# One buffer moved into the weight ring, and a fallback branch that loads its weights in small pieces

## The chip, the core and the metric

The kernel runs on one core of a Trainium2 chip. The metric is the time of one execution on the device in microseconds (us); the kernel before takes 759.27 us, the median of 3 runs (758.9 to 759.5).

## What is computed

A trunk of two layers works on one sequence of 256 tokens with 1024 features, all in float32. Each layer is a token mixer followed by a mixture of experts (MoE), both behind an RMS norm and a modulation by a conditioning vector. Layer 0 mixes with chunked gated linear attention, layer 1 with a gated recurrent block. A router picks two of 16 experts for each token:

```python
for i in range(DEPTH):                       # 2 layers
    sh1, sc1, g1, sh2, sc2, g2 = jnp.split(cond @ ada_w[i] + ada_b[i], 6, axis=-1)
    h = modulate(rmsnorm(x, norm_mix_g[i]), sh1, sc1)
    x = x + g1[:, None] * mixer_i(h)         # gla_mixer or lru_mixer
    h = modulate(rmsnorm(x, norm_ffn_g[i]), sh2, sc2)
    x = x + g2[:, None] * grouped_moe(h, router_w, router_bias, ...)
return rmsnorm(x, final_norm_g)

# grouped_moe, after the choice of two experts per token:
for e in range(N_EXPERTS):                   # 16
    he = jax.nn.silu(t @ w_gate[e]) * (t @ w_up[e])
    out = out + combine[:, e:e + 1] * (he @ w_down[e])
```

Every weight is used once, so some 285 MB have to come from HBM.

## The kernel before

**The ring.** Weights come in pieces of 1 MB (128 partitions x 2048 floats). SP (SyncE) issues them one after the other, in the order in which they are used, into a pool `ring` of `SLOTS = 17` buffers (slots). `Stream` hands them out: `ahead(n)` emits the transfers up to piece n, `get` first calls `ahead(at + look)` and then returns the next piece. A piece's transfer can be issued when a slot is free, that is when the last reader of an earlier piece is done. Some activations live in slots too (`big(...)`: `v`, `S`, `sg`, `oT`, `xp`, `xc`, `xg` and so on), so `look` leaves room for them: 13 in the mixers, 15 in the MoE. The framework that the kernel is written in chooses the slot of each tile, orders each engine's instructions and writes all semaphores.

**`h` and `hT`.** `new_h` makes the normed activations `h` (tokens in partitions) and their transpose `hT` (8 KB in each partition, exactly a slot's size), each in a buffer of its own in the pool `wk`. `hT` is read by the projections of the mixer, and in `out_route` it holds the transposed x from which `logits` computes the router (L830); behind the last `logits` only the overflow branch reads it.

**One layer.** The mixer runs, then `out_route`: output projection, norm, router, and `route_order`, which ranks the experts by their token counts. The ranking (`r_ordi`, L951) is read into registers of SP; before that only the weights of two experts with fixed places (unit `u0`, 12 pieces) can be transferred. `moe` then works through seven units: six with two experts and 12 pieces each, and the last one with four experts and 24 pieces. A unit does `up_proj` (gate and up, L1030), `down_proj` (L1041; in the last unit `down_part`, L1052) and `scatter` (L1060, L1061).

**The overflow branch.** Each expert has a fixed number of places for tokens. If some expert got more tokens than places, `overflow` repairs the sum. It is called once in each layer, in the sixth unit (`u == len(UNITS) - 2`). SP reads the flag behind the last transfer emitted by then (`issue_after(mark["load"])`), and every engine compares and branches (L1067). In the body a loop over 16 experts loads whole halves of the three weights into `h` (six transfers of 1 MB on SP in one pass) and computes with `hT`. On the measured inputs the flag is 0 in both layers and the body is skipped. An `If` is a barrier to the order: nothing behind it in the program goes ahead of it on the same engine.

**The completion counters.** SP's transfers use eight semaphores in turn, one for each transfer in order; a transfer's counter is full when all its data has landed. Where a branch is skipped, each engine still has to bring the counters that the body would have raised to the values that the code behind the branch expects. For a transfer counter of the body, the skipping path on SP holds one instruction: it waits until the transfers issued before on that counter have landed, and adds what the body would have added.

Of the kernel before, what the change touches and what calls it, by code (L numbers as in the profile page):

```python
# [14 lines left out]
P = 128  # L15
# [20 lines left out]
]  # L36
NS = 2
ND = NE - NS
SLOTS = 17
HALVES = [slice(0, 512), slice(512, 1024)]  # L40

TAIL = [(slice(0, 512), 0), (slice(512, 768), 0), (slice(768, 1024), 1024)]
# [33 lines left out]
def trunk(ctx, tc, I, out):  # L76
# [5 lines left out]
    wk = ctx.enter_context(tc.tile_pool(name="wk", bufs=1))  # L82
    sm = ctx.enter_context(tc.tile_pool(name="sm", bufs=2))
    pp = ctx.enter_context(tc.tile_pool(name="pp", bufs=8, space=PSUM))
    stream = Stream(ring, SLOTS - 4)

    def bank():
        return pp.tile([P, 512], F32, name="ps")

    def big(name):  # L90
        return ring.tile([P, 2048], F32, name="w")

    def mid(name):
        return wk.tile([P, 1024], F32, name="mid", tag="mid", bufs=3)
# [313 lines left out]
        return rsqrt(ss)  # L408

    def new_h():  # L410
        return wk.tile([P, NM, D], F32, name="h"), wk.tile([P, 8, S], F32, name="hT")

    def scaled(h, m, r):

# [45 lines left out]
    def out_route(l, yT, gate, gs, rest=None, last=None):  # L460

        w = [stream.get("o").rearrange("p (j n) -> p j n", j=2) for _ in range(4)]
        stream.look = SLOTS - 2
        h, hT = new_h()
        R = route_begin()

        def part(m, hf, between={}):
            sl = slice(hf * 512, (hf + 1) * 512)
            ps = bank()
            for k in range(8):  # L470
                if k in between:
                    between[k]()
                T.matmul(ps, yT[:, k, m * P:(m + 1) * P], w[k // 2][:, k % 2, sl], start=k == 0, stop=k == 7)  # L473
            tmp = s2("tmp")
            V.tensor_mul(tmp, ps, gate[:, sl])
            b = V.tensor_add(x[:, m, sl], x[:, m, sl], tmp)
            mark["x"] = b.ins

        def first():
            turn_h(x, hT, 0, halves=[1])  # L480
            stats_of[0] = stats(0)
            scaled(h, 0, stats_of[0])

        late = len(jobs) > 2
        stats_of = [None, None]
        with tc.manual_schedule(engines={T.engine}):
            part(0, 0)
            part(0, 1, {3: lambda: turn_h(x, hT, 0, halves=[0])})
            if rest:
                rest()  # L490
            router(R, gs)
            part(1, 0, {2: lambda: settle(2), 4: first, 6: lambda: router_shift(R, gs[1], 0), 7: lambda: logits(R, hT, 0)})
            router_shift(R, gs[1], 1)
            scores(R, 0, stats_of[0])
            choose(R, 0)
            fill(2)
            part(1, 1, {3: lambda: turn_h(x, hT, 1, halves=[0]), 5: lambda: logits(R, hT, 1, halves=[0]),
                        7: lambda: route_count(R, 0)})
            stream.ahead(stream.at + SLOTS - 1)
            r = stats(1)  # L500
            if late:
                accs = mid("acc")
                fill_now(accs[:, 0:512])
            else:
                settle(1)
            turn_h(x, hT, 1, halves=[1])
            xg, oh = gather_begin(R)
            gather_tile(R, h, oh, 0, 0, [0])
            logits(R, hT, 1, halves=[1])
            scores(R, 1, r)  # L510
            scaled(h, 1, r)
            gather_tile(R, h, oh, 0, 0, [1, 2, 3])
            choose(R, 1)
            gather_tile(R, h, oh, 0, 1)
            route_count(R, 1)
            if late:
                fill_now(accs[:, 512:1024])
            else:
                settle(1)
            if last:  # L520
                last()
            gather_end(l, R, h, xg, gs)
        R["xg"] = xg
        return h, hT, R
# [468 lines left out]
    def moe(l, h, hT, R, gs, g2, done=None):  # L993
# [69 lines left out]
        def overflow():  # L1063

            with tc.issue_after(mark["load"]):
                flag = nc.values_load(R["flag"][0:1, 0:1], min_val=0, max_val=1)
            with tc.If(flag > 0):  # L1067
                bent_before = mark["bent"]
                for m in range(NM):
                    turn_h(h, hT, m, gs)  # L1070
                mark["bent"] = bent_before
                co = sm.tile([P, NM, NE], F32, name="o_co", bufs=1)
                c2 = sm.tile([P, NM, NE], F32, name="o_c2", bufs=1)
                for m in range(NM):
                    V.tensor_scalar(co[:, m], R["oh"][:, m, 0], R["wv"][:, m, 0:1], None, op0=OP.mult)
                    V.scalar_tensor_tensor(c2[:, m], R["oh"][:, m, 1], R["wv"][:, m, 1:2], co[:, m],
                                           op0=OP.mult, op1=OP.add)
                V.tensor_mul(co, c2, R["ov"])
                with tc.For_i(0, NE, 1) as e:
                    def load(name, n, j, q):  # L1080
                        t = h.rearrange("p m n -> p (m n)")
                        nc.sync.dma_start(t, I[name][l][ds(e, 1), q * n:(q + 1) * n, :]
                                          .rearrange("o (p j) n -> (o p) (j n)", j=j))
                        return t.rearrange("p (j n) -> p j n", j=j)

                    cc = sm.tile([P, NM], F32, name="o_cc", bufs=1)
                    V.tensor_copy(cc[:, :, None], co[:, :, ds(e, 1)])
                    pgu = []
                    for name in ("moe_w_gate", "moe_w_up"):
                        pm = [bank() for _ in range(NM)]  # L1090
                        for q in range(2):
                            w = load(name, 512, 4, q)
                            for m in range(NM):
                                for j in range(4):
                                    k = 4 * q + j
                                    T.matmul(pm[m], hT[:, k, m * P:(m + 1) * P], w[:, j], start=k == 0, stop=k == 7)
                        pgu.append(pm)
                    aTs = []
                    am, tm = mid("o_act"), mid("o_aT")
                    for m in range(NM):  # L1100
                        act = am[:, m * DE:(m + 1) * DE]
                        A.activation(act, pgu[0][m], AF.Silu)
                        V.tensor_mul(act, act, pgu[1][m])
                        ps = bank()
                        av = act.rearrange("t (b p j) -> t b j p", b=2, j=2)
                        for k in range(4):
                            T.transpose(ps[:, k * P:(k + 1) * P], av[:, k // 2, k % 2, :], ident)
                        aT = tm[:, m * DE:(m + 1) * DE].rearrange("p (k t) -> p k t", k=4)
                        A.copy(aT, ps.rearrange("p (k t) -> p k t", k=4))
                        aTs.append(aT)  # L1110
                    py = [[bank() for _ in range(2)] for _ in range(NM)]
                    for q in range(2):
                        w = load("moe_w_down", 256, 2, q)
                        for m in range(NM):
                            for hf in range(2):
                                for j in range(2):
                                    k = 2 * q + j
                                    T.matmul(py[m][hf], aTs[m][:, k], w[:, j, hf * 512:(hf + 1) * 512],
                                             start=k == 0, stop=k == 3)
                    for m in range(NM):  # L1120
                        for hf in range(2):
                            sl = slice(hf * 512, (hf + 1) * 512)
                            tmp = am[:, hf * 512:(hf + 1) * 512]
                            V.scalar_tensor_tensor(tmp, py[m][hf], cc[:, m:m + 1], g2[:, sl], op0=OP.mult, op1=OP.mult)
                            V.tensor_add(x[:, m, sl], x[:, m, sl], tmp)

        xg = R["xg"]
        with tc.issue_after(mark["bent"]):
            route_end(R, *R["order"])
        pend = None  # L1130
        for u, unit in enumerate(UNITS):
            y = mid("y")
            t0 = (u - 1) % 2 * P if u else 0
            if u == len(UNITS) - 2:
                scatter(*pend)
                pend = None
                overflow()
            pg = up_proj(unit, xg, t0)
            if u:
                settle()  # L1140
# [49 lines left out]
    h, hT, R = out_route(0, oT, g1, gf, rest)  # L1190
    ss0 = sm.tile([P, 3, NM], F32, name="ss3", bufs=1)
    moe(0, h, hT, R, gf, g2, done=lambda q: last_squares(q, ss0))
    stream.look = SLOTS - 4
    h, hT = norm(rsqrt2(ss0), gn)
    g1 = gate_vec(1, 0)
    gf = scale_shift(1, 1)
# [52 lines left out]
```

## Time and profile of the kernel before

| | |
|---|---|
| time, median of 3 runs | 759.27 us (758.9 to 759.5) |
| time of the profiled execution | 757.96 us |
| its span, first to last instruction | 756.2 us |
| TensorE busy / VectorE busy / ScalarE busy | 93% / 45% / 17% |
| HBM read over the span | 284.54 MB, mean 379 GB/s with the rest |

The profile covers one execution. Its span is cut into 40 equal slices; for each slice a digit tells how busy an engine or the transfer engines were, and a line gives the GB/s that the transfers moved. Matmuls are pipelined, so a busy TensorE is not one at its peak. "DMA share" is the mean busy share of the 16 transfer engines; it can be a little over 1.

### The profile page before, as it was taken

Reading aid. Unit: us, or ns where it says so; the run is one execution under the profiler, and the core shown is the slowest. Engines: PE = TensorE matmul, PEld = TensorE weight load, DVE = VectorE, ACT = ScalarE, POOL = GpSimd, SP = SyncE. Lnnn points to the kernel's source line nnn. Section 1 sums busy time; section 2 is a strip of 40 time slices with the busy share of each in tenths; the row PEclk is TensorE's granted clock in tenths of the full one; section 3 lists DMA queues with packets and bytes.
Section 4 is the critical chain, followed back from the end, with each engine's and each line's share of the span. In section 5 each row is a group of like instructions: output and inputs, shape, how many; then the busy total and the mean of one; then the engine's idle time right before and its main releaser. Section 6 shows DMA issues by size and latency. Waiting matters only on the chain. (4 is left out here: it accounts for less than half of the span.)

```text
span 756.2 us, 9538 instructions
## 1 busy us (share of the span) xinstructions
PE 699.6 (93%) x3559; PEld 342.8 (45%) x3559; DVE 340.4 (45%) x780; ACT 131.4 (17%) x257; POOL 27.4 (4%) x69
## 2 busy tenths in 40 slices
PE   4899899999999999999887999998999999999874
PEld 3345745454633533533226888655433433433212
DVE  3626983897413223231023589996523143140214
ACT  5006112122200000000013166123210010010002
POOL 5000001000000000000000014000000000000000
PEclk9999999999999999999999999999999999999998
DMA  9999999779999999999999999991999999999994
GB/s 304 384 386 387 386 396 386 269 318 384 423 370 422 421 421 420 423 409 422 411 363 379 381 367 350 406 377 59 423 421 419 419 421 421 421 420 410 422 373 150
DMA packets 80445, 286.27 MB, mean 379 GB/s; under 512 B 5991, under 2 KB 16280, under 8 KB 57866
## 3 DMA queue, kind: packets, MB, share of 16 engines
q1 hardware_dynamic: 78752, 284.71, 96.0%
q10 hardware_dynamic: 1258, 0.66, 0.3%
q8 instruction: 30, 0.49, 0.3%
q0 software_dynamic: 384, 0.23, 0.1%
q14 instruction: 21, 0.17, 0.1%
HBM read 284.54 MB, written 1.05 MB: 378 GB/s over the span
## 5 line engine op out<-in xcount | busy, mean ns | idle before, releaser
L1030 PE MATMUL ps<-w 128*32 128x512 f32 (+1 forms) x1280 | 204.1, 593 | 9.6 <-DMA w<-in_moe_w_up_dram 7.4
L1030 PEld LDWEIGHTS ps<-w 128*32 128x32 f32 (+1 forms) x1280 | 61.8, 121 | 148.7 <-issue 121.7
L1041 PE MATMUL ps<-w,s 128*32 128x512 f32 (+1 forms) x512 | 85.0, 594 | 2.7 <-ACT s L1160 2.7
L1147 DVE TENSOR_TENSOR s<-s,ps 128x512 f32<-128x512 f32 x14 | 9.6, 688 | 149.6 <-PE ps L1030 149.6
L1061 DVE TENSOR_TENSOR x<-x,ps 128x512 f32<-128x512 f32 (+1 forms) x60 | 39.1, 652 | 59.7 <-PE ps L1060 59.7
L317 DVE SCALAR_TENSOR_TENSOR acc<-w,cond,acc 128x512 f32<-128x512 f32 x84 | 64.8, 794 | 1.1
L473 PE MATMUL ps<-w 128*128 128x512 f32 x128 | 59.3, 599 | 0.0
L1060 PE MATMUL ps<-mid,s 128*128 128x512 f32 (+1 forms) x120 | 55.1, 581 | 2.9 <-DVE mid L1168 2.6
L740 PE MATMUL ps<-hT,w 128*128 128x256 f32 x256 | 55.7, 379 | 0.0
L1041 PEld LDWEIGHTS ps<-w,s 128*32 128x32 f32 (+1 forms) x512 | 25.6, 123 | 58.3 <-issue 50.9
L740 PEld LDWEIGHTS ps<-hT,w 128*128 128x128 f32 x256 | 48.7, 191 | 6.7 <-ACT hT L423 0.2
L1179 DVE TENSOR_TENSOR mid<-ps,gate 128x512 f32<-128x512 f32 x24 | 16.6, 692 | 64.7 <-PE ps L1041 64.7
L561 PE MATMUL ps<-w,hT 128*128 128x512 f32 x96 | 42.5, 596 | 1.8 <-DVE hT L425 1.0
L904 PE MATMUL ps<-onehot,h 128*128 128x256 f32 x192 | 42.4, 379 | 0.0
L317 DVE SCALAR_TENSOR_TENSOR gate<-w,cond,gate 128x512 f32<-128x512 f32 x56 | 40.9, 748 | 0.9
L1146 ACT ACTIVATE s<-ps 128x512 f32<-128x512 f32 x14 | 8.4, 597 | 183.6 <-PE ps L1030 183.6
L904 PEld LDWEIGHTS ps<-onehot,h 128*128 128x128 f32 x192 | 36.4, 190 | 7.0 <-issue 2.4
L1060 PEld LDWEIGHTS ps<-mid,s 128*128 128x128 f32 x120 | 20.5, 190 | 30.8 <-issue 20.1
L1160 ACT COPY s<-ps 128x512 f32<-128x512 f32 x14 | 8.2, 586 | 147.2 <-PE ps L1158 147.2
L529 PE MATMUL ps<-w,hT 128*128 128x512 f32 x64 | 29.6, 619 | 3.7 <-DVE w L637 3.7
L473 PEld LDWEIGHTS ps<-w 128*128 128x128 f32 x128 | 22.8, 191 | 20.7 <-issue 18.9
L561 PEld LDWEIGHTS ps<-w,hT 128*128 128x128 f32 x96 | 17.8, 190 | 23.9 <-issue 21.0
(261 smaller groups left out, 602.5 us busy)
## 6 DMA issues: line engine op xcount, KB each, us to landing
w<-in_moe_w_gate_dram SPq DMA_DIRECT2D x64, 1024.0 KB, 11.2
w<-in_moe_w_up_dram SPq DMA_DIRECT2D x64, 1024.0 KB, 15.7
w<-in_moe_w_down_dram SPq DMA_DIRECT2D x56, 1024.0 KB, 17.8
w<-in_ada_w_dram SPq DMA_DIRECT2D x48, 1024.0 KB, 13.5
w<-in_gla_w_in_dram SPq DMA_DIRECT2D x12, 1024.0 KB, 14.6
w<-in_moe_w_down_dram SPq DMA_DIRECT2D x16, 512.0 KB, 9.5
w<-in_lru_w_in_dram SPq DMA_DIRECT2D x8, 1024.0 KB, 12.5
w<-in_gla_w_out_dram SPq DMA_DIRECT2D x4, 1024.0 KB, 12.5
```

Of the source, the lines that this page charges most:

```text
L317: V.scalar_tensor_tensor(acc, w, cond[:, k:k + 1], acc, op0=OP.mult, op1=OP.add)
L473: T.matmul(ps, yT[:, k, m * P:(m + 1) * P], w[k // 2][:, k % 2, sl], start=k == 0, stop=k == 7)
L529: T.matmul(ps, hT[:, k, m * P:(m + 1) * P], w[k // 4][:, k % 4, :], start=k == 0, stop=k == 7)
L561: T.matmul(pst[i][m], hT[:, 4 * b + j, m * P:(m + 1) * P], w[:, j], start=b == 0 and j == 0, stop=b == 1 and j == 3)
L740: T.matmul(ps[:, 0:S], w[k // 4][:, k % 4, ct * P:(ct + 1) * P], hT[:, k, :], start=k == 0, stop=k == 7)
L904: T.matmul(ps[j // 2][:, j % 2 * 2 * P:(j % 2 + 1) * 2 * P], hv[:, b, j, :], oh, start=m == 0 and j % 2 == 0, stop=m == 1 and j % 2 == 1, ...
L1030: T.matmul(ps[p0:p0 + n], xg[:, k, t0 + p0:t0 + p0 + n], w[i][:, j, :], start=k == 0, stop=k == 7)
L1041: T.matmul(ps[hf][p0:p0 + n], aT[:, k, p0:p0 + n], w[i][:, j, hf * 512:(hf + 1) * 512], start=k == 0, stop=k == 3)
L1060: T.matmul(ps, wt[:, m * P:(m + 1) * P], y[:, sl], start=True, stop=True)
L1061: V.tensor_add(x[:, m, sl], x[:, m, sl], ps)
L1147: V.tensor_mul(act, act, pu)
L1179: V.tensor_mul(y[:, sl], py[hf], g2[:, sl])
```

## The change

`SLOTS` becomes 18 and `hT` a `big` tile of the ring; its own buffer in `wk` is gone. All counts that leave room in the ring are lowered by one, so that they keep their values (13 in the mixers, 15 and 16 in `out_route`), but inside `moe` `look` becomes `SLOTS - 2 = 16` (before 15) until the last unit, where it is 15 as before. Since `hT` may be overwritten in the MoE, the overflow branch no longer reads it: it transposes `h` again inside its loop, into a `mid` tile, and it no longer loads into `h`: the weights come in pieces of 256 KB into the two small buffers named `acc`. One pass of its loop now holds 48 transfers: for each of the two token halves 8 for gate, 8 for up and 2 x 4 for down.

```diff
-SLOTS = 17
+SLOTS = 18
...
-    stream = Stream(ring, SLOTS - 4)
+    stream = Stream(ring, SLOTS - 5)
...
-        return wk.tile([P, NM, D], F32, name="h"), wk.tile([P, 8, S], F32, name="hT")
+        return wk.tile([P, NM, D], F32, name="h"), big("hT").rearrange("p (k t) -> p k t", k=8)
...
-        stream.look = SLOTS - 2
+        stream.look = SLOTS - 3
         h, hT = new_h()
...
-            stream.ahead(stream.at + SLOTS - 1)
+            stream.ahead(stream.at + SLOTS - 2)
...
             with tc.If(flag > 0):
-                bent_before = mark["bent"]
-                for m in range(NM):
-                    turn_h(h, hT, m, gs)
-                mark["bent"] = bent_before
...
                 with tc.For_i(0, NE, 1) as e:
-                    def load(name, n, j, q):
-                        t = h.rearrange("p m n -> p (m n)")
-                        nc.sync.dma_start(t, I[name][l][ds(e, 1), q * n:(q + 1) * n, :]
-                                          .rearrange("o (p j) n -> (o p) (j n)", j=j))
+                    def load(name, b, j, js, sl):
+                        t = sm.tile([P, 512], F32, name="acc", bufs=2)
+                        n = P * js
+                        nc.sync.dma_start(t, I[name][l][ds(e, 1), b * n:(b + 1) * n, sl]
+                                          .rearrange("o (p j) n -> (o p) j n", j=js)[:, j, :])
+                        return t
...
+                    for m in range(NM):
+                        hv = h[:, m, :].rearrange("t (b j p) -> t b j p", b=2, j=4)
+                        for b in range(2):
+                            ps = bank()
+                            for j in range(4):
+                                T.transpose(ps[:, j * P:(j + 1) * P], hv[:, b, j, :], ident)
+                            for j in range(4):
+                                bent(tT[:, 4 * b + j], ps[:, j * P:(j + 1) * P], 4 * b + j, gs)
+                        pgu = []
+                        for name in ("moe_w_gate", "moe_w_up"):
+                            pm = bank()
+                            for k in range(8):
+                                T.matmul(pm, tT[:, k], load(name, k // 4, k % 4, 4, slice(0, 512)), start=k == 0, stop=k == 7)
+                            pgu.append(pm)
...
+                        for sl in HALVES:
+                            py = bank()
+                            for k in range(4):
+                                T.matmul(py, aT[:, k], load("moe_w_down", k // 2, k % 2, 2, sl), start=k == 0, stop=k == 3)
...
         xg = R["xg"]
+        stream.look = SLOTS - 2
...
                 overflow()
+            if u + 1 == len(UNITS):
+                stream.look = SLOTS - 3
+            y = mid("y")
             pg = up_proj(unit, xg, t0)
...
-    stream.look = SLOTS - 4
+    stream.look = SLOTS - 5
```

## Rows read from the trace of the kernel before

**Rows 1.** The page's 40 slices of the span: share and rate of transfers.

```profile
DMA  9999999779999999999999999991999999999994
GB/s 304 384 386 387 386 396 386 269 318 384 423 370 422 421 421 420 423 409 422 411 363 379 381 367 350 406 377 59 423 421 419 419 421 421 421 420 410 422 373 150
```

**Rows 2.** The chain that ended last: start us, us, what.

```profile
677.10 14.00 PE ps L1030 x64
...
717.40 15.24 DMA w<-in_moe_w_down_dram
...
732.68 5.33 PE ps L1052 x26
```

**Rows 3.** TensorE's waits for transfers, 355:400, then 680:745: total us, times, longest.

```profile
PE ps L1030 <- DMA w<-in_moe_w_up_dram: 3.3, 3, 1.5
PE ps L1052 <- DMA w<-in_moe_w_down_dram: 2.8, 3, 1.7
...
PE ps L1030 <- DMA w<-in_moe_w_up_dram: 4.1, 4, 1.5
```

**Rows 4.** SP's waits, 178:215, and its next issue: start us, us.

```profile
SPq L255 <- PE ps L1041: 16.7, 2, 14.9
...
210.38 0.34 SPq L255 DMA_DIRECT2D w<-in_moe_w_gate_dram  x1
```

**Rows 5.** Stretches: us, busy by engine, granted clock, DMA share, GB/s.

```profile
210.00:211.00 1.00, 1.00 (x6) 0.29 (x4) 0.00 (x0) 0.00 (x0) 0.00 (x0) 1.00 0.26 107
211.00:212.00 1.00, 1.00 (x8) 0.38 (x6) 0.00 (x0) 0.00 (x0) 0.00 (x0) 1.00 0.68 131
212.00:213.00 1.00, 1.00 (x8) 0.33 (x6) 0.02 (x1) 0.00 (x0) 0.00 (x0) 1.00 0.84 344
...
210.00:220.00 10.00, 10.00 (x78) 2.98 (x78) 2.60 (x5) 0.00 (x0) 0.00 (x0) 1.00 0.88 324
```

**Rows 6.** Line L1067 on SP, layer 0, then two events of layer 1.

```profile
L1067 SPq EVENT_SEMAPHORE  x6: 17/17/17, 332.0 to 334.8; - x6
L1067 SPq COMPARE_BRANCH  x1: 53/53/53, 325.7 to 325.7; - x1
...
L1067 SPq EVENT_SEMAPHORE  x1: 17/17/17, 678.5 to 678.5; - x1
L1067 SPq EVENT_SEMAPHORE  x1: 17/17/17, 681.0 to 681.0; - x1
```

**Rows 7.** SP's issues just before and just behind the branch, both layers.

```profile
323.85 1.49 SPq L255 DMA_DIRECT2D w<-in_moe_w_gate_dram  x2
335.96 0.34 SPq L255 DMA_DIRECT2D w<-in_moe_w_gate_dram  x1
...
669.21 1.49 SPq L255 DMA_DIRECT2D w<-in_moe_w_gate_dram  x2
682.27 0.34 SPq L255 DMA_DIRECT2D w<-in_moe_w_gate_dram  x1
```

**Rows 8.** An issue into empty queues, and the stretches in which its data starts.

```profile
527.42 2.69 SPq L255 DMA_DIRECT2D w<-in_moe_w_gate_dram  x4
...
529.00:529.50 0.50, 0.50 (x6) 0.16 (x4) 0.31 (x1) 0.42 (x2) 0.00 (x0) 1.00 0.50 180
529.50:530.00 0.50, 0.50 (x6) 0.21 (x4) 0.43 (x2) 0.48 (x3) 0.00 (x0) 1.00 1.12 475
```

**Rows 9.** The one stretch of layer 0's branch with a lower share.

```profile
337.00:338.00 1.00, 1.00 (x8) 0.43 (x6) 0.00 (x0) 0.00 (x0) 0.00 (x0) 1.00 0.76 295
```

**Rows 10.** The router's order, its first readers' stretch, and `hT` in layer 0's `out_route`.

```profile
L951 DVE CAST r_ordi<-r_ordf x2: 161/163/165, 177.4 to 526.4; 1x14 int32<-1x14 f32 x2
...
520.00:530.00 10.00, 8.62 (x51) 5.57 (x52) 7.29 (x38) 4.15 (x9) 0.00 (x0) 1.00 0.14 39
...
L435 ACT COPY hT<-ps x2: 586/586/587, 142.1 to 161.2; 128x512 f32<-128x512 f32 x2
L830 PE MATMUL ps<-r_rw,hT x32: 179/262/283, 154.8 to 171.2; 128*128 128x16 f32 x32
```

More of the change, by code (lines that the diff above doesn't have):

```diff
@@ L1079, in overflow @@
                 with tc.For_i(0, NE, 1) as e:
-                    def load(name, n, j, q):
-                        t = h.rearrange("p m n -> p (m n)")
-                        nc.sync.dma_start(t, I[name][l][ds(e, 1), q * n:(q + 1) * n, :]
-                                          .rearrange("o (p j) n -> (o p) (j n)", j=j))
-                        return t.rearrange("p (j n) -> p j n", j=j)
+                    def load(name, b, j, js, sl):
[4 more added lines that the diff above has]
+                        return t
@@ L1086, in overflow @@
+                    bent_before = mark["bent"]
                     cc = sm.tile([P, NM], F32, name="o_cc", bufs=1)
                     V.tensor_copy(cc[:, :, None], co[:, :, ds(e, 1)])
[L1088 to L1097, printed above, removed]
@@ L1098, in overflow @@
-                    aTs = []
-                    am, tm = mid("o_act"), mid("o_aT")
-                    for m in range(NM):
-                        act = am[:, m * DE:(m + 1) * DE]
-                        A.activation(act, pgu[0][m], AF.Silu)
-                        V.tensor_mul(act, act, pgu[1][m])
+                    tT, am = mid("o_hT").rearrange("p (k t) -> p k t", k=8), mid("o_act")
+                    for m in range(NM):
+                        hv = h[:, m, :].rearrange("t (b j p) -> t b j p", b=2, j=4)
[11 more added lines that the diff above has]
+                            pgu.append(pm)
+                        act, aT = am[:, 0:DE], am[:, DE:].rearrange("p (k t) -> p k t", k=4)
+                        A.activation(act, pgu[0], AF.Silu)
+                        V.tensor_mul(act, act, pgu[1])
@@ L1107, in overflow @@
                             T.transpose(ps[:, k * P:(k + 1) * P], av[:, k // 2, k % 2, :], ident)
-                        aT = tm[:, m * DE:(m + 1) * DE].rearrange("p (k t) -> p k t", k=4)
                         A.copy(aT, ps.rearrange("p (k t) -> p k t", k=4))
[L1110 to L1125, printed above, removed]
+                        for sl in HALVES:
+                            py = bank()
+                            for k in range(4):
+                                T.matmul(py, aT[:, k], load("moe_w_down", k // 2, k % 2, 2, sl), start=k == 0, stop=k == 3)
+                            V.scalar_tensor_tensor(act, py, cc[:, m:m + 1], g2[:, sl], op0=OP.mult, op1=OP.mult)
+                            V.tensor_add(x[:, m, sl], x[:, m, sl], act)
+                    mark["bent"] = bent_before
         xg = R["xg"]
+        stream.look = SLOTS - 2
         with tc.issue_after(mark["bent"]):
@@ L1131, in moe @@
         for u, unit in enumerate(UNITS):
-            y = mid("y")
             t0 = (u - 1) % 2 * P if u else 0
```

## The prediction

> **What bounds the kernel now.** I read the page's strip of 40 slices first, because a ring of weight buffers can only matter where transfers stop. Transfers are busy nearly everywhere [rows 1]: some 420 GB/s in both MoE stages, 385 in the mixers (smaller pieces). At 421 GB/s a piece of 1 MB (1.0486 million bytes) takes 2.49 us, and two events of SP that each wait for one landing lie 2.5 us apart [rows 6], which is the same. So in the MoE the transfers set the pace: TensorE waits for them at the end of both MoE stages [rows 3], and the chain that ended last runs through transfers that were queued for 15 us before they landed, with 5.3 us of matmuls behind them [rows 2]. A microsecond in which the queues are empty in a MoE stage therefore moves the stage's end by a microsecond; a piece that is merely issued earlier moves nothing. The ring stops SP often, but only where the queues run dry does that cost.
>
> Three places matter for this change: the dip at 210 us in layer 0's MoE, the overflow branch in both layers (325 and 671 us), and the stretch before the router's order, where the transfers of layer 1 stand nearly still [rows 1, 10].
>
> **The eighteenth slot.** While `hT` is alive the change gives nothing: one slot more, one tenant more, and the reserves keep their values. `hT` is dead from the last `logits` (L830, up to 171.2 us [rows 10]) to the next norm, so the gain is one more piece in flight in the MoE. In layer 0 SP stood 14.9 us before it could issue at 210.38 [rows 4], waiting for TensorE to release a slot of the first unit. Meanwhile the queues ran dry: 0.74, 0.32 and 0.16 us of the microseconds from 210 to 213 are missing, 1.2 us together [rows 5]. With a piece of 2.49 us issued ahead of that wait the hole closes: **-1.2 us**. Its bounds are 0 (the slot goes unused) and -2.3 us, what the rate of 324 GB/s over the whole ten microseconds lacks against 421 [rows 5]. In layer 1 the MoE's slices stand at 419 to 423 GB/s until the branch [rows 1], so the same slot finds nothing to fill.
>
> Between the last use of the old `hT` and the first write of the new one at 142.1 us [rows 10] a piece can also go out sooner. That brings nothing: what ends this stage is the order of the experts, written at 177.4 and 526.4 us [rows 10] by VectorE, and the known pieces have been issued before; earlier pieces only make the idle time before the order longer.
>
> **The branch.** Its body is not executed, so its transposes, its 48 loads and its products cost nothing as such. The skipping path does cost. In layer 0 SP branches at 325.7 us and then executes six semaphore events, until 334.8 [rows 6]: one for each of the six transfers in the loop's body, each waiting for a landing on its counter. The pieces issued last before the branch, two at 323.85 and after, and two at 669.21 and after [rows 7], sit on the two counters that are not among the six. They are what feeds the queues while SP stands. The check on this: in layer 1 the last event passes a landing at 681.0; the two newest pieces need 2 x 2.49 us more and land near 686, yet SP issues at 682.27 [rows 6, 7]. So before, SP goes on with two pieces, 5 us of work, still queued, and the cost is a dip: 0.24 us in layer 0 [rows 9].
>
> With 48 transfers in one pass, the body uses all eight counters, so the skipping path waits on all eight: for **every** piece that SP has issued, the newest included. When SP may go on, the queues are empty. Behind SP's wait stand all further pieces, and for these TensorE waits at the stage's end. The price of one such drain, step by step:
> - From the last landing to the next issue: 681.0 to 682.27 [rows 6, 7], 1.3 us. It holds two short events, the flag and the next expert's number.
> - From an issue into empty queues until data flows: SP issues at 527.42, when the share was near nothing; 0.50 from 529.0 to 529.5, full from there on [rows 8]. So the flow starts at about 529.25: 1.8 us.
> - The engines don't stop at the same instant; from the 0.26 in the microsecond at 210 [rows 5] I estimate 0.5 us of their time before the last landing.
>
> That makes 3.6 us for each layer. No row shows a drain in the MoE behind a branch, so the ends: 1.8 us, if the engines' overlap and SP's preparation hide all but the flow's start, and 5 us, if the run-out is a full 2 us. I take 3.6 because two of its three parts are read directly. The old dip of 0.24 us goes away with it, in each layer.
>
> TensorE has some 14 pieces in SBUF at that moment, and eight of them take it 14.0 us (gate and up of a unit) [rows 2], so for some 25 us it does not notice; but the stream is behind by 3.4 us from then on and TensorE meets that at the end of the stage [rows 3].
>
> The Trainium skill has a smaller price for the flow's start: in "DMA: Bandwidth & Descriptors", section "Latency and other measured facts", a transfer issued through SP shows its first byte after some 0.6 us. By that each drain would be 2.4 us, and the total 762.4. The row at 527.42 shows three times as much here, and I go by the row.
>
> **The rest.** `y = mid(...)` behind the branch and the reserve of the last unit change no order that is executed. TensorE, VectorE and ScalarE skip the branch as before, with one event each. `hT` in layer 0's `out_route` now has to find a slot at 142.1 us, when pieces of the stream want them too; its first reader runs at 154.8 [rows 10], so up to 12 us are covered, and I cost it at nothing. Without that cover it is the third rival.
>
> **The sum.** Against the profiled execution's own time of 757.96 us: layer 0 -1.2 + 3.6 - 0.24, layer 1 + 3.6 - 0.24, together +5.5: 763.5. The median of the runs lies 1.3 us higher than the profiled time; carried over, 759.27 + 5.5 gives **764.8 us**, +0.7%. With all lower ends, 2 x 1.56 - 2.3, it is 760.1; with all upper ends, 2 x 4.76, it is 768.8.
>
> **Rivals.**
> - *The skipping path does not drain* (the other side). If the loop's 48 transfers were kept on few counters, or the wait were moved into the body, SP would go on with pieces queued as now. Then only the gain stays: 759.27 - 1.2 = 758.1, at most 757.0. It decides at the point where the newest piece's counter is not among those waited for. Against it: before, six transfers gave exactly six events in each layer [rows 6].
> - *The first drain is absorbed.* In layer 1 the transfers are nearly idle for some 16 us before the order [rows 1, 10]; if the stage from 400 us to the order ran on its own clock, layer 0's loss and its gain would both vanish there: 759.27 + 3.4 = 762.6. Against it: TensorE waits for transfers at the end of layer 0's MoE [rows 3], and the mixer of layer 1 starts from that end, so the order moves with it.
> - *`hT` waits for its slot.* SP's slots near 150 us are released by slow work; should `hT` get one only after 155 us, the router's logits would start 2 to 6 us late and with them the order: 767 to 771.
> - *The slot stays unused* (the change does not do what it says): no gain, 766.0.
>
> **How the numbers follow.** Chances: the forecast 0.68, the unused slot 0.04, the absorbed drain 0.10, the waiting `hT` 0.06, no drain 0.12. The range, 760.1 to 769.0, takes in the bounds of the sum and all cases but no drain and the far half of the third rival. A measurement of this kernel can tell about 0.2%, 1.5 us, from no change. No drain lies at the edge of that, 758.1 with 757.0 as its best: 0.05 of it faster, 0.07 the same. All others are slower by more: 0.88.
>
> **What would show it.** In the profile after: eight events of SP at the branch's line instead of six, the last one at the landing of the newest piece; SP's next issue some 16 us behind its branch (before, in layer 0, 10 us); behind it a hole of 2 us or more in the transfer share in both layers; no hole at 210 us; the order in layer 0 within a microsecond of 177.4, and in layer 1 some 2 us later than 526.4. Wrong would be six or fewer events, or a hole that the stage's end does not show.

## The result, and the profile after the change

The changed kernel takes **782.41 us** (median of 4 runs, 781.88 to 782.79), beside 759.38 us for the kernel before (758.9 to 761.2) in the same series. The ratio is 1.0296, 95% interval 1.0273 to 1.0318. The prediction was 764.8 us with a range up to 769.0: the sign was right, the size was not, and the time lies 13 us outside the range.

The profiled execution has a span of 780.3 us (before 756.2). To see where the 24.1 us of difference come from, I cut both spans at four events that the two traces share: the router's order in each layer (`r_ordi`, L951) and the start of the last down product of each MoE (L1052). All columns are us of one profiled execution; e1, e2, e4 and e12 are experiments of the next section.

| stretch | before | after | e1 | e2 | e4 | e12 |
|---|---|---|---|---|---|---|
| start to order, layer 0 | 177.4 | 186.2 | 180.2 | 184.4 | 177.3 | 178.7 |
| order to end of MoE, layer 0 | 222.5 | 225.6 | 227.5 | 220.0 | 226.3 | 220.1 |
| to order, layer 1 | 126.5 | 133.2 | 126.5 | 134.5 | 126.5 | 126.4 |
| order to end of MoE, layer 1 | 219.5 | 224.7 | 226.0 | 220.2 | 224.8 | 219.4 |
| rest | 10.2 | 10.7 | 10.7 | 10.3 | 10.7 | 10.3 |

Two kinds of loss stand side by side: in the MoE (+3.1 and +5.2 us, with the slot's gain in the first) and, not in the forecast's sum, ahead of both orders (+8.8 and +6.7 us). The page's strip of rates shows the first kind: the twelfth slice, which holds the old hole, is whole now (420, before 370), and two slices at the branches stand at 318 and 320, where [rows 1] has 409 and 410.

```profile
GB/s 290 387 387 386 387 399 373 265 325 235 424 420 421 420 422 420 422 318 389 410 363 378 383 387 398 421 264 1 373 420 420 420 420 422 421 419 320 422 375 147
```

**The slot.** The hole of [rows 5] began 32.6 us behind the order of layer 0. The order comes 8.8 us later now, so the place to look is 219 us (columns: us, busy time and count of PE, PEld, DVE, ACT, POOL, granted clock, DMA share, GB/s):

```profile
219.00:229.00 10.00, 10.00 (x82) 2.99 (x82) 2.60 (x5) 0.00 (x0) 0.00 (x0) 1.00 1.01 419
```

The hole is closed. Over the ten microseconds 419 GB/s stand against 324, which is 10 x (419 - 324) / 421 = 2.3 us of transfers gained: the upper bound of the prediction, not its 1.2.

**The branch.** Line L1067 on SP, which answers to [rows 6], then the part of it at 349 us:

```profile
L1067 SPq EVENT_SEMAPHORE  x16: 17/17/17, 339.8 to 708.1; - x16
L1067 SPq COMPARE_BRANCH  x2: 53/53/53, 334.5 to 689.7; - x2
...
L1067 SPq EVENT_SEMAPHORE  x3: 17/17/17, 349.8 to 349.9; - x3
```

Sixteen events are eight in each layer, as predicted. SP's next issue, and the windows of both layers around it:

```profile
351.14 2.15 SPq L255 DMA_DIRECT2D w<-in_moe_w_gate_dram  x4
...
709.23 2.75 SPq L255 DMA_DIRECT2D w<-in_moe_w_gate_dram  x5
```

```profile
345.00:346.00 1.00, 1.00 (x7) 0.37 (x5) 0.00 (x0) 0.00 (x0) 0.00 (x0) 1.00 0.84 352
346.00:347.00 1.00, 1.00 (x8) 0.49 (x6) 0.00 (x0) 0.00 (x0) 0.00 (x0) 1.00 0.53 221
347.00:348.00 1.00, 1.00 (x7) 0.35 (x5) 0.00 (x0) 0.01 (x1) 0.00 (x0) 1.00 0.12 49
348.00:349.00 1.00, 1.00 (x7) 0.36 (x5) 0.00 (x0) 0.59 (x1) 0.00 (x0) 1.00 0.08 33
349.00:350.00 1.00, 1.00 (x8) 0.49 (x6) 0.00 (x0) 0.00 (x0) 0.00 (x0) 1.00 0.00 0
...
352.00:353.00 1.00, 1.00 (x8) 0.49 (x6) 0.00 (x0) 0.00 (x0) 0.00 (x0) 1.00 0.86 147
353.00:354.00 1.00, 1.00 (x8) 0.36 (x5) 0.00 (x0) 0.00 (x0) 0.00 (x0) 1.00 0.88 360
...
705.00:706.00 1.00, 1.00 (x8) 0.50 (x6) 0.00 (x0) 0.00 (x0) 0.00 (x0) 1.00 0.73 303
706.00:707.00 1.00, 1.00 (x6) 0.40 (x4) 0.00 (x0) 0.00 (x0) 0.00 (x0) 1.00 0.43 180
707.00:708.00 1.00, 1.00 (x8) 0.48 (x6) 0.00 (x0) 0.00 (x0) 0.00 (x0) 1.00 0.06 25
...
710.00:711.00 1.00, 0.28 (x2) 0.00 (x0) 0.61 (x1) 0.00 (x0) 0.00 (x0) 1.00 0.64 123
```

Here the rate is the better measure: the share counts an engine as busy while its first data is still on the way (0.86 at 147 GB/s). Against 421 GB/s layer 0 lacks 0.16 + 0.48 + 0.88 + 0.92 + 3 x 1 + 0.65 + 0.14 = 6.2 us; layer 1, with 0.10 missing in the microsecond before 705 and all of 708 to 710, lacks 4.6. The drain has the three parts of the prediction, but the first is much longer than it said. Up to the last landing (349.7, 708.0) 3.1 and 1.9 us are lost while some engines have already run out of work and others have not; from there to the next issue 1.4 and 1.2; the rest, 1.7 and 1.5, until data flows.

**`hT`.** Its two copies ahead of the first logits in each layer (L435), the order, TensorE's waits for the copies, and the windows behind the waits:

```profile
L435 ACT COPY w<-ps x1: 583/583/583, 152.2 to 152.2; 128x512 f32<-128x512 f32 x1
L435 DVE COPY w<-ps x1: 670/670/670, 160.5 to 160.5; 128x512 f32<-128x512 f32 x1
...
L951 DVE CAST r_ordi<-r_ordf x2: 164/164/164, 186.2 to 545.0; 1x14 int32<-1x14 f32 x2
```

```profile
PE ps L830 <- DVE w L435: 4.3, 1, 4.3
...
PE ps L830 <- DVE w L435: 3.4, 1, 3.4
```

```profile
160.00:170.00 10.00, 8.77 (x23) 5.07 (x24) 7.44 (x26) 0.21 (x1) 0.00 (x0) 0.66 0.94 375
...
520.00:530.00 10.00, 10.00 (x26) 5.64 (x27) 3.61 (x20) 1.42 (x4) 0.00 (x0) 0.68 0.39 162
```

Before, these copies ran at 142.1 (ACT, [rows 10]) and 153.3 (DVE). Now they run at 152.2 and 160.5. What VectorE did meanwhile, in order of time (start, us):

```profile
153.81 2.75 DVE L317 SCALAR_TENSOR_TENSOR acc<-w,cond,acc 128x512 f32<-128x512 f32 x4
...
156.54 4.04 DVE L317 SCALAR_TENSOR_TENSOR acc<-w,cond,acc 128x512 f32<-128x512 f32 x6
160.51 0.67 DVE L435 COPY w<-ps 128x512 f32<-128x512 f32 x1
```

VectorE did not wait for a slot here. It was busy with ten products of `fill` (low-priority work on the modulation vectors), and the copy stands behind them in its written order; before, it stood behind one. So the order of the instructions changed (e3 shows what changed it), TensorE waited 4.3 and 3.4 us, and at each wait its granted clock falls to the lower level, 1.2 GHz: 0.66 and 0.68 on average are 3.4 and 3.2 us of TensorE's time that are missing from the ten microseconds.

### The profile page after: what moved, and what is told of

Read it like the earlier page. It is cut to its first block, busy times and chain, and to the rows that moved or that the text cites. A ratio compares the mean times of both kernels' runs of the same rounds, so it can differ in the third digit from the quotient of the medians.

```text
span 780.3 us, 9552 instructions
## 1 busy us (share of the span) xinstructions
PE 711.9 (91%) x3559; PEld 349.8 (45%) x3559; DVE 342.8 (44%) x780; ACT 134.7 (17%) x259; POOL 23.3 (3%) x69
## 5 line engine op out<-in xcount | busy, mean ns | idle before, releaser
L1030 PE MATMUL ps<-w 128*32 128x512 f32 (+1 forms) x1280 | 209.3, 603 | 13.3 <-DMA w<-in_moe_w_up_dram 10.8
L1030 PEld LDWEIGHTS ps<-w 128*32 128x32 f32 (+1 forms) x1280 | 64.8, 122 | 154.3 <-issue 123.3
L473 PE MATMUL ps<-w 128*128 128x512 f32 x128 | 63.5, 635 | 0.0
L740 PE MATMUL ps<-w 128*128 128x256 f32 x256 | 56.1, 380 | 0.5 <-ACT w L423 0.5
L740 PEld LDWEIGHTS ps<-w 128*128 128x128 f32 x256 | 48.7, 191 | 7.5 <-ACT w L423 1.0
L561 PE MATMUL ps<-w 128*128 128x512 f32 x96 | 43.9, 614 | 1.0 <-DVE w L425 1.0
L473 PEld LDWEIGHTS ps<-w 128*128 128x128 f32 x128 | 24.2, 204 | 22.0 <-issue 20.2
L529 PE MATMUL ps<-w 128*128 128x512 f32 x64 | 29.8, 623 | 3.7 <-DVE w L637 3.7
L561 PEld LDWEIGHTS ps<-w 128*128 128x128 f32 x96 | 18.5, 196 | 23.8 <-issue 22.6
## 6 DMA issues: line engine op xcount, KB each, us to landing
w<-in_lru_w_in_dram SPq DMA_DIRECT2D x8, 1024.0 KB, 13.5
```

Source lines behind the costliest of these rows:

```text
L529: T.matmul(ps, hT[:, k, m * P:(m + 1) * P], w[k // 4][:, k % 4, :], start=k == 0, stop=k == 7)
L561: T.matmul(pst[i][m], hT[:, 4 * b + j, m * P:(m + 1) * P], w[:, j], start=b == 0 and j == 0, stop=b == 1 and j == 3)
L740: T.matmul(ps[:, 0:S], w[k // 4][:, k % 4, ct * P:(ct + 1) * P], hT[:, k, :], start=k == 0, stop=k == 7)
L1030: T.matmul(ps[p0:p0 + n], xg[:, k, t0 + p0:t0 + p0 + n], w[i][:, j, :], start=k == 0, stop=k == 7)
```

## The experiments

The kernel before ran beside each series: 759.17 us for e1 to e4, 759.63 for e5 to e8 (with the runs before), 759.85 for e9 to e12.

**e1: the branch alone.** The kernel before with the new branch, its loop of 48 transfers and the `y` that goes with it; all else as before.

```diff
+                    def load(name, b, j, js, sl):
+                        t = sm.tile([P, 512], F32, name="acc", bufs=2)
...
```

> The kernel before, with the new overflow branch and nothing else (17 slots, hT in its own buffer). First theory (each drain costs some 3.4 us, and the rest of the loss comes from where hT lives): eight semaphore events on SP at the branch in both layers, order at 177.4 in layer 0, time 759.4 + 2 x 3.4 = about 766. Rival (the branch is nearly the whole loss, by drains that later stages multiply): 775 or more, with TensorE's clock falling in the router's stage as well.

Measured: 771.25 us, ratio 1.0141 (1.0112 to 1.0170). Sixteen events on SP (334.8 to 695.2), no late copy, the stretch to layer 1's order at its old 126.5 us. So the branch costs 12 us by the medians (10.7 by the ratio), not the 7 I expected and not the whole. The order of layer 0 lies 2.8 us later than before although the program is the same up to the branch: TensorE's clock falls to the lower level after an idle of 3.7 us near 95 us in some executions and for different times. The window 90:100 of this run shows 0.77, that of e7 1.00:

```profile
90.00:100.00 10.00, 6.30 (x28) 3.84 (x25) 9.39 (x38) 0.93 (x1) 0.00 (x0) 0.77 1.05 387
```

```profile
90.00:100.00 10.00, 6.30 (x21) 3.03 (x19) 9.42 (x38) 0.00 (x0) 0.00 (x0) 1.00 1.05 387
```

The clock is 3.4 us of the difference (0.77 here and 0.89 in the next ten microseconds of e1, 1.00 in both of e7); the same program brings the order at 175.6 us in e7 and at 180.2 in e1. A single profile's first stretch is therefore uncertain by 4.6 us, and the medians and the later stretches carry the comparisons below.

**e2: all but the drains.** The changed kernel with the loop's transfers issued by POOL.

```diff
-                        nc.sync.dma_start(t, I[name][l][ds(e, 1), ...
+                        nc.gpsimd.dma_start(t, I[name][l][ds(e, 1), ...
```

> The changed kernel, with the branch's 48 transfers issued by POOL instead of SP, so that the skipping path on SP has no transfer counter to wait for. First theory: no event of SP at the branch waits for a landing, no hole in the transfers there, and the two drains' 3.4 to 3.8 us each are back: 782.4 - 7 = about 775; the late order of layer 0 (186 us) and the late start stay. Rival (the branch is nearly the whole loss): 760 or less.

Measured: 771.52 us, ratio 1.0160 (1.0136 to 1.0185): 10.9 us under the changed kernel, where I had put 7 on the two drains. SP only branches at L1067, and the window behind shows the transfers going on:

```profile
L1067 SPq COMPARE_BRANCH  x2: 45/49/53, 332.7 to 683.6; - x2
```

```profile
340.00:345.00 5.00, 5.00 (x26) 2.02 (x24) 0.24 (x1) 0.00 (x0) 0.00 (x0) 1.00 1.02 419
```

The stages ahead of both orders keep their loss (table). Branch and `hT` are two separate causes.

**e3: `hT` ahead of the pieces.** The changed kernel with one line in `out_route`, ahead of the four `get("o")`:

```diff
+        stream.look = SLOTS - 9
```

> The changed kernel; only the reserve ahead of the four pieces of the output projection is raised (look 9 in place of 13), so that no further piece asks for a slot before hT does. First theory (hT gets its slot behind pieces that were asked for earlier, so its copies stand later in the static order, TensorE waits for them and then runs at half its clock): the copies of hT stand ahead of the gate products again, TensorE's waits of 4.3 and 3.4 us at the first logits and the half clock behind them go, the order comes some 7 us earlier in each layer, 782.4 - 14 = about 768. Rival (the clock falls there for another reason, or fewer pieces in flight cost as much as hT gains): the order stays within 2 us of 186, time 778 or more.

Measured: 768.88 us, ratio 1.0116 (1.0093 to 1.0139): 13.5 us under the changed kernel. Both copies stand early again, with no wait of TensorE for them in layer 0 and 0.5 us in layer 1, as in the kernel before. Layer 0's copies run at 143.9 (ACT) and 155.0:

```profile
L435 DVE COPY w<-ps x1: 681/681/681, 155.0 to 155.0; 128x512 f32<-128x512 f32 x1
```

With `look` at 13 the four `get` ask for further pieces ahead of `hT`; without these requests its copies keep their old place. The ring is as large and its tenants are the same, so it was standing behind these requests that delayed `hT`. Why the framework then moved the copies behind other work is inferred from the order that came out; no run shows how it decides.

**e4: and an early start.** e3, and the first piece asked for before the first norm asks for `hT`. In the changed kernel SP waits 3.1 us for a transfer of ScalarE's queue whose counter it needs (here both queues draw on the same eight counters), and issues its first piece at 5.18 us. Its row among the waits of SP in the first 9 us:

```profile
SPq L196 <- DMA tab<-in_ada_b_dram: 3.1, 1, 3.1
```

```diff
+    stream.ahead(1)
     oT, rest = gla(gs)
```

> As the run before (hT ahead of pieces), and the first weight piece is asked for before the first norm asks for hT. First theory (the first piece is issued 3 us late because its slot is handed out behind hT's, and its counter is then one that a transfer of ScalarE's queue still holds): SP's first piece is issued at about 2.1 us in place of 5.2, everything behind it comes 1.2 us earlier, time 1.2 us under the run before, about 767. Rival (the start is hidden behind the mixer's transfers or TensorE's own work): the same as the run before within 0.4 us.

Measured: 768.06 us, ratio 1.0114 (1.0093 to 1.0136). The first piece goes out at 2.14 us again, and the order comes 1.8 us earlier than in e3, which a single profile can't tell from chance; the medians differ by 0.8 us, inside their scatter. What is left over before is the branch, less the slot's gain.

**e5, e12, e10, e11: the repaired kernel and its parts.** e5 and e12 are one kernel: e4 with the branch's transfers on POOL. e10 is the kernel before with the new branch on POOL; e11 is e12 without `stream.ahead(1)`.

> The changed kernel with all three repairs: hT asked for ahead of the pieces, the first weight piece ahead of hT, and the branch's transfers on POOL. First theory (the loss is two drains of some 5.6 us, the late copies of hT, and the start; what is left is the eighteenth slot's gain of 2.3 us and the old dips of 0.3 us): the transfers lose nothing at the branch, order at 177.3, 759.3 - 2.3 - 0.6 = about 756.5, faster by 0.3 to 0.4%. Rival (in layer 1 the slot's tenants delay the router as well, or TensorE's own work sets the end once the transfers are earlier): 759 to 760, no gain.

> The kernel before (17 slots, hT in its own buffer) with the new branch and its transfers on POOL: neither a drain nor an eighteenth slot. First theory: the old dips at the branch go (0.3 us each), the dip at 210 us stays, 759.4 - 0.6 = 758.8, within 0.2% of before. Rival (moving the transfers to POOL is what made the repaired kernel faster, not the slot): as fast as the repaired kernel, 757.5 or less.

> The repaired kernel without the repair of the start: SP's first piece at about 5.2 us again. First theory: 1.2 to 1.8 us over the repaired kernel, about 759.3, no longer faster than before. Rival (the late start is hidden): equal to the repaired kernel within 0.5 us.

> The repaired kernel once more (hT ahead of the pieces, first weight piece ahead of hT, branch on POOL), to stand beside the two others in one series. First theory: 757 to 758 against 759.5, 1.5 to 2.5 us under the kernel before with the branch on POOL, which lacks the slot; no dip at 210 us. Rival (the slot's gain is used up later): the two are equal within 0.5 us.

Measured: e5 757.92 us, ratio 0.9977 (0.9964 to 0.9991); e12 757.69, 0.9975 (0.9963 to 0.9987); e10 759.07, 0.9991 (0.9979 to 1.0004); e11 758.78, 0.9983 (0.9971 to 0.9995). The repaired kernel takes 0.25% less than the kernel before, and neither interval reaches 1. Against e10 the slot, with all that moved with it, is worth 1.4 us, less than the 2.3 us that the transfers gain, and the late start costs 1.1 us. The intervals of e10, e11 and e12 overlap, so both figures are rough. The first theory's 756.5 for e5 was too low by 1.4 us, 0.9 of them because the slot's gain does not all arrive in the time. The dip at 210 us is gone in e12 (first window, 424 GB/s) and there in e10 (second, 336):

```profile
210.00:220.00 10.00, 10.00 (x72) 3.02 (x72) 2.60 (x5) 0.00 (x0) 0.00 (x0) 1.00 1.02 424
```

```profile
210.00:220.00 10.00, 10.00 (x70) 3.07 (x70) 2.60 (x5) 0.00 (x0) 0.00 (x0) 1.00 0.90 336
```

**e6, e9: TensorE kept busy while it waits.** The changed kernel with products that nobody reads between the two halves of the first logits: e6 as below, e9 with `range(5 - l)`.

```diff
+            def keep():
+                ps = bank()
+                for _ in range(10 - 2 * l):
+                    T.matmul(ps, yT[:, 0, 0:P], w[0][:, 0, 0:512], start=True, stop=True)
```

> The changed kernel with ten (layer 0) and eight (layer 1) extra products of 128x512, whose result nobody reads, between the two halves of the first logits, where TensorE waits 4.3 and 3.4 us for hT. They take 0.43 us each, as much as the wait. First theory (the granted clock falls because of the wait, and the half clock behind it costs some 3.3 us in each layer): no half clock in the router's stage, order some 3 us earlier in each layer, 782.4 - 6.5 = about 776, though the wait itself stays filled and brings nothing. Rival (the clock falls there for another reason, or the stage behind it doesn't depend on TensorE's clock): half clock as before, 782 or a little more.

> As the run that kept TensorE busy, but with five and four extra products in place of ten and eight: each is carried out as two passes of 0.43 us, so the first attempt overfilled the waits of 4.3 and 3.4 us by as much again. First theory (half clock behind the wait costs 3.3 us in layer 0 and nearly as much in layer 1): granted clock 1.00 behind the wait in both layers, from the second half of the first logits to the order 21.7 us as in the kernel before (25.0 in the changed kernel), time 782.4 - 6 = about 776. Rival (the stage behind the wait gains nothing from TensorE's clock): 782.

Measured: e6 784.1 us (1.0332, 1.0307 to 1.0356); e9 775.6 us (1.0216, 1.0191 to 1.0241). In e6 the expectation failed because I had sized the filling wrongly: each product shows as two matmuls in the trace, so ten took 8.8 us and the logits resumed at 166.0, 4.8 us later than in the changed kernel. In e9 five and four fit the waits, and the time falls by 6.8 us though TensorE does more work. The same ten microseconds as above, in e9, then its chain of TensorE (start, us; L495 are the five products, L836 the second half of the first logits):

```profile
160.00:170.00 10.00, 10.00 (x42) 5.87 (x42) 5.59 (x25) 1.42 (x4) 0.00 (x0) 1.00 0.98 383
```

```profile
154.94 4.54 PE L495 MATMUL ps<-w 128*128 128x512 f32 x10
159.42 1.06 PE L836 MATMUL ps<-r_rw,w 128*128 128x16 f32 x8
...
161.69 2.84 PE L473 MATMUL ps<-w 128*128 128x512 f32 x6
```

The same six products took 4.08 us in the changed kernel:

```profile
161.23 1.89 PE L830 MATMUL ps<-r_rw,w 128*128 128x16 f32 x8 [4.31 <-DVE w L435]
...
165.48 4.08 PE L473 MATMUL ps<-w 128*128 128x512 f32 x6
```

From the second half of the first logits to the order it is 186.2 - 161.2 = 25.0 us in the changed kernel and 181.1 - 159.4 = 21.7 in e9; in layer 1 25.0 (from 520.0) and 21.9. So about half of what the late copies cost is the lower clock behind the wait, 3.3 and 3.1 us, and the other half the wait.

**e7, e8: the drain by itself.** The kernel before with its short loop; one or two of its six transfers of 1 MB are cut in half, so that seven or eight counters are waited for: e7 as below, e8 with `q in (0, 1)`.

```diff
+                        if name == "moe_w_down" and q in (1,):
+                            for i in range(2):
+                                nc.sync.dma_start(t[:, i * D:(i + 1) * D], ...[:, i, :])
```

> The kernel before, with one of the six transfers in the branch's loop cut into two, so that one pass holds seven and the skipping path waits on seven counters: one piece stays queued in place of two. First theory (a drain costs 5.6 us, of which 3 us are the run-out of the slower transfer engines, 1.3 from the last landing to the next issue, 1.5 until the data flows; each queued piece covers 2.5 us): 3.1 us in each layer against 0.3 before, 759.3 + 5.6 = about 765. Rival one (no long run-out: 1.3 + 1.8 less 2.5): 0.6 us in each layer, 760. Rival two (the drain's length comes from the new branch's large body): 760 to 761.

> The same with two transfers of the loop cut in two: eight in one pass, all eight counters waited for, in an otherwise short body. First theory (the drain is due to the counters alone, not to the body's size): 5.6 us in each layer, as with 48 transfers, 759.3 + 10.6 = about 770. Rival one (run-out of 0.5 us as in the prediction): 3.6 us in each layer, 766. Rival two (the large body is what makes the branch slow): 762 or less.

Measured: e7 763.68 us, ratio 1.0072 (1.0050 to 1.0094), +4.1 us; e8 767.26 us, 1.0106 (1.0085 to 1.0128), +7.6 us. SP's events at the branch, seven and eight in each layer, then the windows of layer 0, e7 first and e8 behind it:

```profile
L1067 SPq EVENT_SEMAPHORE  x14: 17/17/17, 330.9 to 685.0; - x14
...
L1067 SPq EVENT_SEMAPHORE  x16: 17/17/17, 333.7 to 692.2; - x16
```

```profile
335.00:336.00 1.00, 1.00 (x6) 0.29 (x4) 0.00 (x0) 0.00 (x0) 0.00 (x0) 1.00 0.75 311
336.00:337.00 1.00, 1.00 (x8) 0.34 (x6) 0.00 (x0) 0.00 (x0) 0.00 (x0) 1.00 0.36 147
337.00:338.00 1.00, 1.00 (x8) 0.37 (x6) 0.00 (x0) 0.05 (x1) 0.00 (x0) 1.00 0.10 41
338.00:339.00 1.00, 1.00 (x6) 0.29 (x4) 0.00 (x0) 0.55 (x1) 0.00 (x0) 1.00 0.48 106
339.00:340.00 1.00, 1.00 (x8) 0.34 (x6) 0.00 (x0) 0.00 (x0) 0.00 (x0) 1.00 0.87 344
```

```profile
338.00:339.00 1.00, 1.00 (x8) 0.38 (x6) 0.00 (x0) 0.00 (x0) 0.00 (x0) 1.00 0.79 311
339.00:340.00 1.00, 1.00 (x6) 0.29 (x4) 0.00 (x0) 0.00 (x0) 0.00 (x0) 1.00 0.45 188
340.00:341.00 1.00, 1.00 (x8) 0.34 (x6) 0.00 (x0) 0.00 (x0) 0.00 (x0) 1.00 0.08 33
341.00:342.00 1.00, 1.00 (x8) 0.38 (x6) 0.00 (x0) 0.04 (x1) 0.00 (x0) 1.00 0.00 0
342.00:343.00 1.00, 1.00 (x6) 0.29 (x4) 0.00 (x0) 0.56 (x1) 0.00 (x0) 1.00 0.03 8
343.00:344.00 1.00, 1.00 (x8) 0.33 (x6) 0.00 (x0) 0.00 (x0) 0.00 (x0) 1.00 0.74 106
344.00:345.00 1.00, 1.00 (x8) 0.39 (x6) 0.00 (x0) 0.00 (x0) 0.00 (x0) 1.00 0.55 197
```

Missing against 421 GB/s: 0.3 us with six counters (295 in [rows 9]), 2.7 with seven, 5.0 with eight. Each piece that may stay queued covers 2.3 to 2.4 us, nearly the 2.49 us that it takes. That waiting on all counters is enough for a drain is shown: the body of e8 is nearly as short as before, so rival two falls. Both times lie between the first theory (765 and 770) and rival one (760 and 766). For e8 rival one, a run-out of 0.5 us, lies nearer by the times (3.8 us per layer over before) than by the rates (5.0); the windows of e8 show a run-out of 1.9 us ahead of the landing at 341.2, so the term itself does not hold.

With the loop of 48 the times give more per layer: 5.2 (e4 less e12, halved) to 6.1 (e1 less e10, halved), beside 4.1 (e8 less e10, halved): 1 to 2 us per layer go with the large loop. The rates give less. Over the 25 us behind the branch, against 421 GB/s, transfers worth 5.2 and 5.4 us are missing in e8, 6.0 and 6.4 in e1, 6.2 and 6.1 in e4; that is 0.7 to 1.0 us per layer, and the changed kernel's own 6.4 and 4.9 scatter more widely. Of the rest 0.4 us, once, are the longer stretch in the table's last line. What in the large loop costs this is open.

## Why the prediction was wrong

- **"`hT` in layer 0's `out_route` ... I cost it at nothing": this step failed.** It is 13.5 us (e3), and 12.7 where the branch does not drain (e2 less e11). Its signs failed with it: the order was to stay within a microsecond of 177.4 in layer 0 and to come some 2 us later in layer 1, and came at 186.2 and 18.6 us later. The cover of "up to 12 us" was read from the ACT copy alone, at 142.1 us. The second half of `hT` is VectorE's copy, which the trace of before shows as well:

```profile
153.28 0.69 DVE L435 COPY hT<-ps 128x512 f32<-128x512 f32 x1
```

```profile
154.76 1.85 PE L830 MATMUL ps<-r_rw,hT 128*128 128x16 f32 x16
```

  It ends at 153.97, and the second eight of the sixteen products, which read it, begin near 155.6: 1.6 us of cover, not 12. In layer 1, which the step left out, there was no cover at all: TensorE waited for this copy in the kernel before.

```profile
PE ps L830 <- DVE hT L435: 0.5, 1, 0.5
```

  And I asked only whether a slot would be free in time on the chip. By the order that came out, the slot enters earlier, where the framework fixes the order of instructions: the copy moved behind ten products, 6.8 us together.
- **The third rival** ("`hT` waits for its slot", 767 to 771, chance 0.06) named the place and the sign, but as a stall of 2 to 6 us, once. It happens in both layers, and TensorE's clock falls at each wait (e9: 6.8 us of the 13.5). That a wait of TensorE costs more than its length was in no term.
- **The drains.** That the skipping path waits on eight counters, in both layers, and on the newest piece, came as predicted, and two of the three terms hold (1.3: 1.4 and 1.2; 1.8: 1.7 and 1.5). The term that was mis-sized is the run-out, 0.5 us by the estimate from [rows 5] and 3.1 and 1.9 measured: one microsecond with a share of 0.26 was taken for the whole of it. With it the drain is 6.2 and 4.6 us against 3.6, in layer 0 above the upper end of 5. The medians make the two drains 10.1 (e3 less e11) to 12.2 us (e1 less e10), 3.4 to 5.5 us more than the 6.7 in the sum.
- **The sentence on the Trainium skill** ("DMA: Bandwidth & Descriptors", "Latency and other measured facts", 0.6 us to the first byte): the trace shows 1.5 to 1.7 us lost from the issue until data flows, so the row at 527 was the right one to go by. The same section of the Trainium skill says that two of the sixteen transfer engines are usually slower than the rest. The last shares before layer 0's landing, 0.12 and 0.08 of sixteen, are 1.9 and 1.3 engines still at work, which agrees in number. In layer 1 the last share is 0.06, one engine, and earlier shares, 0.53 in layer 0 (346 us) and 0.43 in layer 1 (706 us), say that half of the engines had run out sooner; so two slow engines are not the whole of it. The windows don't name the engines. The cause that the Trainium skill guesses at concerns software-made descriptors, and the weights' transfers are listed as `hardware_dynamic` in this profile.
- **The slot** gains 2.3 us of transfers where I took 1.2: I had added up missing shares, and [rows 5] show a share of 0.68 at only 131 GB/s. The rate, which I kept as a bound, was the measure: 1.6 us by it in the same three microseconds, the rest behind them. Of the gain 1.4 us arrive in the time (e12 against e10).
- **Not in the sum:** the first piece 3 us later, worth 0.8 to 1.1 us. With `hT` asked for first, the issue order between SP and ScalarE moved, and with it the counters.
- **The absorbed drain** (second rival) fell: with `hT` repaired, the stretch from the end of layer 0's MoE to layer 1's order is 126.5 us in e4, with a drain, and 126.4 in e12, without.

Put together along the repairs: 13.5 (`hT`, e3) + 0.8 (start, e4) + 10.4 (drains, e4 less e12) - 1.9 (e12 against the kernel before, by the ratio) = 22.8 us, against 23.0 measured. These steps follow one another, so they have to add up nearly; what tests them is that the prices repeat in other pairs: the drains cost 10.9 us beside the late `hT` (e2) and 10.1 without it (e3 less e11), `hT` 13.5 beside the drains and 12.7 without them.

## What to carry to other kernels

A buffer that moves into a shared pool is no longer free of charge at the moment of its first write: look up each of its writers, the last one above all, measure its own cover to its own reader in each layer, and ask for the buffer before the requests that can wait. A skipped branch costs the waits on the counters that its body uses, so keep a queue that must not run dry out of the body, or leave it counters that the body doesn't use. Price a wait of TensorE of several microseconds with the lower clock behind it.

## What the runs showed of the hardware

- At a wait of 4.3 us TensorE's granted clock fell to 1.2 GHz, and the same work behind the wait took 3.3 us more; with products in this wait and in layer 1's of 3.4 us it stayed at 1.00, and the kernel became 6.8 us faster (e9). Behind an idle of 3.7 us near 95 us, the same in the executions looked at here (6.3 us busy of ten), it fell in e1 (0.77 on average over 90:100 us) and not in e7 (1.00).
- Queued transfers don't end together: with no further work behind them, the sixteen engines lose 1.9 to 3.1 us of their time before the last landing (the changed kernel; 1.9 in e8).
- Each transfer counter that a skipped branch leaves out kept one piece of 1 MB queued, worth 2.3 to 2.4 us of transfers in layer 0 (0.3, 2.7 and 5.0 us missing with six, seven and eight counters: the kernel before, e7, e8).
